# A mixture of experts: weights split in parts of 2048 columns instead of units of 1024, and in another order

## Chip, cores and metric

The kernel runs on one core of one Trainium2 chip. The metric is the time of one execution in microseconds of the device, as the median of several runs; less is better.

## What is computed

The reference is one inference step of a decoder layer for a prompt of 2048 tokens and 32 sample tokens: a mixer (attention and a state space part), and behind it a mixture of experts. Only the latter is touched by the change. Each token goes to two of 32 experts (one group of four, then two of its eight), and the tokens of an expert are worked in blocks of up to 128 rows:

```python
MOE_BLOCK = 128
...
    def expert_block(args):
        xb, e = args
        hid = jax.nn.silu(xb @ w_gate[e]) * (xb @ w_up[e])
        return hid @ w_down[e]
...
    contrib = ys[dest].astype(jnp.float32) * sg[:, None]
    return jax.ops.segment_sum(contrib, stok, num_segments=t)
```

Here `xb` is 128 x 1024, `w_gate` and `w_up` are 1024 x 512, and `w_down` is 512 x 1024, in float32, so an expert has 1.57 million weights, 6 MB.

## The kernel before

**Products out of high and low parts.** TensorE gets operands of the type float32r. Each float32 operand is split in two: `h` is its copy in that type (a cast on ScalarE, named ACT in the trace), and `l` the rest, `x - h` (a subtraction on VectorE, named DVE). A product is then three matmuls: h by h, h by l, l by h. `split` (L130) does this for tokens and hidden values: `xh, xl` of the block's tokens, `hh, hl` of the hidden values. The weights of an expert are split in the same way, by class `Experts` (L1888): loads of raw weights come in six tiles `raw0` to `raw5` of 128 x 2048 (0 to 3 hold gate and up, 4 and 5 hold down), each loaded by SyncE (SP) in `load_w` (L1874 for gate and up, L1877 for down). Each raw tile is split in two halves, so an expert has 12 units of 1024 columns: units 0 to 7 for the up products, 8 to 11 for the down products. `convert` (L1940 the cast, L1941 the subtraction) splits one unit into one of 16 places, and after the second half of a raw tile it issues the load of the next expert's weights into that tile. On SP this load waits for the subtraction to have read the tile.

**A block.** `block` (L2031) is one block of 128 tokens. TensorE first does the up products of both halves of the hidden columns for k = 0 to 3 (24 matmuls of 128 x 512, L2006), then the rest of half 0 (12). `act(0)` is Silu on ScalarE and the product on VectorE (hid, L2009 and L2010). `turned` transposes the next block's tokens (eight transposes, L1994). Then comes half 1 for k = 4 and 5, the two hid transposes of half 0 (`hidT`, L2014), which need the hid product, half 1 for k = 6 and 7, `act(1)`, the down products of c = 0 (six matmuls, L2023), the two hid transposes of half 1, and the down products of c = 1 to 3 (18). That is 72 matmuls. `store` (L2027) scales the result of the block before out of PSUM and sends it to memory. `prepare` splits the next block's tokens out of PSUM.

**What runs beside it.** An expert with up to 128 tokens has one block (`main`). One with more has up to three further blocks ahead of it (`further`), each under a branch (L2118, L2120, L2122). All of the splitting of the next expert's weights is written into the blocks of this expert as steps between the pieces of `block`: the last two units of this expert (`LATE`, down products c = 2 and 3) and the first four of the next (`EARLY`) go into the first further block, or, where there is none, into `main` under a branch of its own (`alone`, L2086, branch L2087). The other units go into `main` by the table `STEPS`. The order on every engine is the order in which the code is written (a manual schedule), so an instruction that waits holds up all that stands behind it on its engine. The first expert's weights are split ahead of this stage, in the tail of the router, by `late_split`.

Of the kernel before, what the change touches and what calls it, by code (L numbers as in the profile page):

```python
# [12 lines left out]
F32 = mybir.dt.float32  # L13
# [1867 lines left out]

STEPS = (), (0, 1, 2, 3, 4, 5), (6,), (7,), (), (), (8, 9)
EARLY = 0, 1, 2, 3
BOTH, AT0, AT1 = 4, 6, 1
LATE = 10, 11


class Experts:  # L1888
# [3 lines left out]
    UNITS, PLACES = 12, 16  # L1892
# [11 lines left out]
    def split(self, pool, *places):  # L1904

        for i in places:
            self.SP[i] = tuple(pool.tile([128, 1024], F32R, name=f"{nm}{i}") for nm in ("wh", "wl"))

    def load(self, p, i):
# [7 lines left out]
        if i in (0, 2, 5):  # L1917
            self.now = self.K.nc.sync.value_load(self.R.order[0:1, p:p + 1], min_val=0, max_val=31)
# [8 lines left out]
    def unit(self, p, u):  # L1927
        return self.SP[(self.UNITS * p + u) % self.PLACES]

    def convert(self, p, u, hi, lo):  # L1930

        h = u % 2
        raw = self.RAW[u // 2]
        wh, wl = self.unit(p, u)
        if u < 8:
            raw = raw.rearrange("p (j k f) -> p j k f", j=2, k=2)[:, :, h]
            wh, wl = (t.rearrange("p (j f) -> p j f", j=2) for t in (wh, wl))
        else:
            raw = raw[:, 1024 * h:1024 * h + 1024]
        hi(wh, raw)  # L1940
        lo.tensor_tensor(out=wl, in0=raw, in1=wh.bitcast(F32), op=ALU.subtract)  # L1941
        if h:
            self.load(p + 1, u // 2)


def moe(K, I, E, first, h2_d, Y_d, R, TK, last):
# [7 lines left out]
    with ExitStack() as st:  # L1954
        w = st.enter_context(tc.tile_pool(name="mw", bufs=1, reuse_waits="tile"))
        ps = st.enter_context(tc.tile_pool(name="mps", bufs=1, space=PSUM, reuse_waits="tile"))
        E.split(w, *range(8, E.PLACES))
        PT = [ps.tile([128, 4, 128], F32, name=f"pt{i}") for i in range(4)]
        PU = [ps.tile([128, 512], F32, name=f"pu{i}") for i in range(2)]
        PO = [ps.tile([128, 512], F32, name=f"po{i}") for i in range(2)]  # L1960
# [6 lines left out]
        for t in PO:  # L1967
            V.memset(t, 0.0)

        def convert(p, us):  # L1970
            for u in us:
                if p < NE:
                    E.convert(p, u, A.copy, V)
# [22 lines left out]
        def prepare():  # L1996

            for hf in range(2):
                ks = slice(4 * hf, 4 * hf + 4)
                split(K, XH[:, ks], XL[:, ks], PT[hf])  # L2000

        def up(p, hf, ks):
            for k in ks:
                wh, wl = (t.rearrange("p (j f) -> p j f", j=2)[:, :, 256 * hf:256 * hf + 256] for t in E.unit(p, k))
# [12 lines left out]
        def down(p, c):  # L2017
            wh, wl = E.unit(p, 8 + c)
# [6 lines left out]
        def store(col):  # L2025
            for i in range(2):
                A.activation(Y[:, 512 * i:512 * i + 512], PO[i], AF.Copy, scale=R.g[:, col:col + 1])  # L2027
# [3 lines left out]
        def block(p, before, x, steps, label, hint):  # L2031
# [28 lines left out]
            steps[6]()  # L2060
# [5 lines left out]

        def further(p, b):


            steps = [nothing] * 7  # L2070
            if b == 0:
                steps[0] = lambda: convert(p, LATE)
                steps[1] = lambda: convert(p + 1, EARLY)
# [10 lines left out]
        def main(p):  # L2084

            def alone():  # L2086
                with tc.If(blocks[p] <= 128):  # L2087
                    convert(p, LATE)
                    convert(p + 1, EARLY)

            def step(i):
                def run():
                    if i == 0:
                        alone()
                    elif i == 1:
                        gather_second(p + 1)
                    elif i == 2:
                        gather_first(p + 2)
                    convert(p + 1, [u for u in STEPS[i] if u not in EARLY])
                return run  # L2100

            block(p, 64 + p, X0 if p + 1 < NE else None, [step(i) for i in range(7)],
# [199 lines left out]
TK = 2176  # L2302
# [111 lines left out]
```

## Time and profile before

| | us |
|---|---|
| median of 3 runs | 2697.63 (2695.93 to 2702.63) |
| the profiled execution's own time | 2700.0 |
| its span | 2698.3 |
| expert stage, from 1627.3 to 2611.8 | 984.5 |
| TensorE busy in the span | 2441.5 (90%) |
| VectorE busy | 1435.3 (53%) |
| ScalarE busy | 1155.7 (43%) |

The mean granted clock of TensorE over the profiled execution is 0.951 of full speed. Times of the profile are counted from the start of the span. Matmuls overlap in the trace: a busy time of 0.4 us is that of one matmul from its start to its modelled end, while the next one starts 0.23 us later. A row of the timeline can stand for several instructions in a row (x6); what stands in brackets behind it is the time the engine stood idle ahead of it and what released it. `SPq` and `PEq` are the sequencers of SP and TensorE.

### The profile page before, as it was taken

The page shows a single profiled execution, that of the slowest core. Times are in us where ns is not written, and L with a number is a line of the kernel's source. Part 1 is how long each engine was busy: PE and PEld are TensorE (multiplying, and loading weights), DVE is VectorE, ACT ScalarE, POOL GpSimd, SP SyncE. Part 2 cuts the span into 40 slices and gives each one's busy share as a digit, 9 for nine tenths or more (in the row PEclk, how much of TensorE's full clock was granted, in tenths as well). Part 3 has the DMA queues.
Part 4 walks back from the last instruction along what each step waited for, and adds up shares of the span by engine and source line. Part 5 has one row for each costly group of instructions (what it writes and reads, how often), then busy time and mean ns, then how long its engine had stood idle before and what let it go on. Part 6 is the DMA issues. An engine that isn't in the chain of part 4 may idle for free. (4 is left out here: it accounts for less than half of the span.)

```text
span 2698.3 us, 36856 instructions
## 1 busy us (share of the span) xinstructions
PE 2441.5 (90%) x12135; PEld 1903.2 (71%) x12135; DVE 1435.3 (53%) x2977; ACT 1155.7 (43%) x1889; POOL 541.9 (20%) x712
## 2 busy tenths in 40 slices
PE   7999899897879999997999958999999999999987
PEld 3766677664457789996677736777777777777763
DVE  4444311256053566563677765537447566667528
ACT  3222211143143445645444435536446556666522
POOL 1022100001001334443344411111111111111103
PEclk9999999798889998998999968999999999999998
DMA  7322311466753632113433336547558577778657
GB/s 278 85 107 99 108 59 51 150 223 193 221 155 116 192 94 63 34 33 105 132 125 125 110 128 252 179 172 288 185 216 304 191 268 261 290 293 316 226 215 292
DMA packets 239281, 467.76 MB, mean 173 GB/s; under 512 B 87764, under 2 KB 117636, under 8 KB 236943
## 3 DMA queue, kind: packets, MB, share of 16 engines
q1 hardware_dynamic: 211496, 411.95, 44.2%
q0 software_dynamic: 16304, 38.50, 4.0%
q10 hardware_dynamic: 11200, 13.83, 1.5%
q8 instruction: 144, 2.36, 0.3%
q14 instruction: 137, 1.12, 0.1%
HBM read 395.60 MB, written 88.44 MB: 179 GB/s over the span
## 5 line engine op out<-in xcount | busy, mean ns | idle before, releaser
L1941 DVE TENSOR_TENSOR wl<-raw,wh 128x1024 fp32r<-128x1024 f32 x384 | 450.2, 1221 | 178.4 <-ACT wh L1940 177.8
L1940 ACT CAST wh<-raw 128x1024 fp32r<-128x1024 f32 x384 | 381.1, 1049 | 75.5 <-SPq L2118 58.8
L2006 PE MATMUL pu<-wh,xh 128*128 128x512 f32 x816 | 333.3, 408 | 20.8 <-PEq L2118 15.0
L2006 PE MATMUL pu<-wh,xl 128*128 128x512 f32 x816 | 323.1, 396 | 1.3 <-issue 1.3
L2006 PE MATMUL pu<-wl,xh 128*128 128x512 f32 x816 | 322.5, 395 | 0.0
L2028 POOL DMA_INDIRECT Y_d<-y,Rdst x52 | 66.8, 1285 | 764.9 <-ACT y L2027 731.6
L206 PE MATMUL po<-wh,hh 128*128 128x512 f32 x512 | 209.3, 409 | 12.1 <-ACT hh L133 12.1
L206 PE MATMUL po<-wl,hh 128*128 128x512 f32 x512 | 207.5, 405 | 0.0
L206 PE MATMUL po<-wh,hl 128*128 128x512 f32 x512 | 203.1, 402 | 0.0
L2006 PEld LDWEIGHTS pu<-wh,xh 128*128 128x128 f32 x816 | 154.5, 189 | 64.2 <-issue 34.3
L2006 PEld LDWEIGHTS pu<-wh,xl 128*128 128x128 f32 x816 | 154.3, 189 | 35.8
L873 DVE CUSTOM_DVE_ANT_0 jk<-pa,mask 128x256 bf16<-128x256 f32 (+1 forms) x384 | 118.0, 362 | 113.6 <-PE pa L870 112.7
L2006 PEld LDWEIGHTS pu<-wl,xh 128*128 128x128 f32 x816 | 154.6, 189 | 30.3
L2023 PE MATMUL po<-wh,hh 128*128 128x512 f32 x408 | 165.0, 404 | 0.0
L2023 PE MATMUL po<-wl,hh 128*128 128x512 f32 x408 | 160.5, 393 | 0.0
L2023 PE MATMUL po<-wh,hl 128*128 128x512 f32 x408 | 160.4, 393 | 0.0
L216 ACT COPY ob<-po 128x512 f32<-128x512 f32 x64 | 37.6, 587 | 266.2 <-PE po L206 264.3
L939 PE MATMUL pb<-QS,KH 128*128 128x256 f32 (+1 forms) x384 | 150.7, 399 | 0.0
L942 ACT ACTIVATE PT<-pb 128x512 f32<-128x512 f32 (+1 forms) x152 | 89.9, 591 | 122.2 <-PE pb L940 118.9
L940 PE MATMUL pb<-QM,KL 65*128 65x256 f32 (+1 forms) x384 | 139.6, 371 | 1.4 <-DMA QM<-MR 1.4
L2010 DVE TENSOR_TENSOR hid<-hid,pu 128x256 f32<-128x256 f32 x102 | 42.6, 417 | 184.1 <-ACT hid L2009 184.1
L988 PE MATMUL pw<-PT,vb 128*128 128x128 f32 (+1 forms) x752 | 132.1, 312 | 0.0
(588 smaller groups left out, 4973.4 us busy)
## 6 DMA issues: line engine op xcount, KB each, us to landing
raw<-w_expert_gate SPq DMA_DIRECT2D x128, 512.0 KB
raw<-w_expert_up SPq DMA_DIRECT2D x128, 512.0 KB
raw<-w_expert_down SPq DMA_DIRECT2D x64, 1024.0 KB
y<-Y_d SPq DMA_DIRECT2D x32, 512.0 KB
kr<-cache_k_win SPq DMA_DIRECT2D x56, 256.0 KB
kr<-cache_v_win SPq DMA_DIRECT2D x56, 256.0 KB
vb<-out_vp SPq DMA_DIRECT2D x96, 128.0 KB
wada<-w_ada_ffn SPq DMA_DIRECT2D x24, 512.0 KB
```

The costliest lines, as they stand in the source:

```text
L206: nc.tensor.matmul(out, a[:, kt, :], wt[c][:, kt], start=(kt == 0 and i == 0), stop=(kt == 7 and i == len(terms) - 1))
L873: V.tensor_tensor_reduce(out=jk[:, o:o + n], in0=pt[:, o:o + n], in1=mask[:, 256 - n:256], op0=ALU.add, op1=ALU.max, scale=1.0, scalar=-3e ...
L939: nc.tensor.matmul(po, cols(KH, c0, step, 128), cols(QS, c0, step, nq), start=True, stop=False)
L940: nc.tensor.matmul(po, cols(KL, c0, step, 128), cols(QM, c0, step, nq), start=False, stop=True)
L942: A.activation(PT[:, :o], ps[:, :o], AF.Exp)
L988: nc.tensor.matmul(out, vt[h, b, idx], PT[:, o + q0:o + q0 + n_], start=start, stop=(final and Wd == W), skip_group_check=True)
L1940: hi(wh, raw)
L1941: lo.tensor_tensor(out=wl, in0=raw, in1=wh.bitcast(F32), op=ALU.subtract)
L2006: nc.tensor.matmul(PU[hf], x[:, k, :], y, start=(k == 0 and j == 0), stop=(k == 7 and j == 2))
L2010: V.tensor_tensor(out=HID[hf], in0=HID[hf], in1=PU[hf][:, 256:512], op=ALU.mult)
L2023: nc.tensor.matmul(PO[i], x[:, c % 2, :], y[:, cs], start=(c == 0 and j == 0), stop=(c == 3 and j == 2))
L2028: nc.gpsimd.indirect_dma_start(out=Y_d, out_offset=bass.IndirectOffsetOnAxis(ap=R.dst[:, col:col + 1], axis=0), in_=Y, in_offset=None, bou ...
```

## The change

An expert's weights are split in six whole parts of 2048 columns, one per raw tile, into eight places, by one cast (`hi`) and one subtraction (`lo`) each. The tables of steps are replaced by four functions in `main`:

- `begin`: under the branch, parts 5 (of this expert), 0 and 1 (of the next). `further` does the same in its first block.
- `second`, ahead of the rest of half 0: the cast of part 2.
- `first`, behind the transposes of the next tokens: the subtraction of part 2, and the load into its tile.
- `end`, behind the second hid transposes: part 3 with its load, and part 4 without.

The load for part 4 is issued behind the next expert's branch L2118 and its further blocks, just ahead of its `main`. `AT0` goes from 6 to 7, so the first hid transposes stand behind three more up matmuls. `prepare` moves from ahead of the first down products to behind the second hid transposes, and splits all 1024 columns at once; `store` scales them at once. The loads for parts 4 and 5 each read the expert's number again. `late_split` does a whole part at every second call.

```diff
-STEPS = (), (0, 1, 2, 3, 4, 5), (6,), (7,), (), (), (8, 9)
-EARLY = 0, 1, 2, 3
-BOTH, AT0, AT1 = 4, 6, 1
-LATE = 10, 11
+LATE, EARLY = 5, (0, 1)
+BOTH, AT0, AT1 = 4, 7, 1
...
-    UNITS, PLACES = 12, 16
+    PARTS, PLACES = 6, 8
...
-        if i in (0, 2, 5):
+        if i in (0, 2, 4, 5):
             self.now = self.K.nc.sync.value_load(self.R.order[0:1, p:p + 1], min_val=0, max_val=31)
...
-        if h:
-            self.load(p + 1, u // 2)
...
+    def hi(self, p, i):
+        self.K.nc.scalar.copy(self.part(p, i)[0], self.RAW[i])
+
+    def lo(self, p, i):
+        wh, wl = self.part(p, i)
+        self.K.nc.vector.tensor_tensor(out=wl, in0=self.RAW[i], in1=wh.bitcast(F32), op=ALU.subtract)
...
+        def convert(p, *parts, hi=True, lo=True, load=True):
+
+            for i in parts:
                 if p < NE:
-                    E.convert(p, u, A.copy, V)
+                    if hi:
+                        E.hi(p, i)
+                    if lo:
+                        E.lo(p, i)
+                        if load:
+                            E.load(p + 1, i)
...
-            for hf in range(2):
-                ks = slice(4 * hf, 4 * hf + 4)
-                split(K, XH[:, ks], XL[:, ks], PT[hf])
+            split(K, XH, XL, PX)
...
-            for i in range(2):
-                A.activation(Y[:, 512 * i:512 * i + 512], PO[i], AF.Copy, scale=R.g[:, col:col + 1])
+            A.activation(Y, PY, AF.Copy, scale=R.g[:, col:col + 1])
...
             up(p, 1, range(AT0, 8))
-            steps[3]()
             act(1)
-            steps[4]()
-            if x is not None:
-                prepare()
-            steps[5]()
...
             hidT(1)
-            steps[6]()
+            if x is not None:
+                prepare()
+            steps[3]()
...
+        def early(p):
+            convert(p, LATE)
+            convert(p + 1, *EARLY)
...
-            def alone():
+            def begin():
                 with tc.If(blocks[p] <= 128):
-                    convert(p, LATE)
-                    convert(p + 1, EARLY)
...
+            def second():
+                gather_second(p + 1)
+                convert(p + 1, 2, lo=False)
+
+            def first():
+                gather_first(p + 2)
+                convert(p + 1, 2, hi=False)
+
+            def end():
+                convert(p + 1, 3)
+                convert(p + 1, 4, load=False)
...
+            if 0 < p:
+                E.load(p + 1, 4)
             main(p)
```

How this moves instructions shows at three places. The names: `wh`, `wl` with a number are the halves or parts of the split weights (`wh6` and `wh7` of before are the halves of part 3, `wh8` and `wh9` those of part 4, `wh10` is the first half of part 5), `hid` the hidden values, `pu` the PSUM of the up products, `px` (before `pt0` and `pt1`) that of the transposed tokens. The order lists don't tell when something runs.

The first place is VectorE in a last block, from the hid product of half 0 to the end. Before:

```order
L2010 TENSOR_TENSOR hid_13306<-hid_13306,pu0_13297 128x256
L1941 TENSOR_TENSOR wl6_12946<-raw3_12788,wh6_12945 128x1024
L134 TENSOR_TENSOR hl0_13308<-pt2_13295,hh0_13307 128x256
L1941 TENSOR_TENSOR wl7_12948<-raw3_12788,wh7_12947 128x1024
L2010 TENSOR_TENSOR hid_13306<-hid_13306,pu1_13298 128x256
L134 TENSOR_TENSOR xl_13302<-pt0_13293,xh_13301 128x512
L134 TENSOR_TENSOR xl_13302<-pt1_13294,xh_13301 128x512
L134 TENSOR_TENSOR hl1_13310<-pt3_13296,hh1_13309 128x256
L1941 TENSOR_TENSOR wl8_13278<-raw4_12791,wh8_13277 128x1024
L1941 TENSOR_TENSOR wl9_13280<-raw4_12791,wh9_13279 128x1024
```

And now:

```order
L2011 TENSOR_TENSOR hid_13280<-hid_13280,pu0_13272 128x256
L1939 TENSOR_TENSOR wl2_12942<-raw2_12785,wh2_12941 128x2048
L134 TENSOR_TENSOR hl0_13282<-pt2_13270,hh0_13281 128x256
L2011 TENSOR_TENSOR hid_13280<-hid_13280,pu1_13273 128x256
L134 TENSOR_TENSOR hl1_13284<-pt3_13271,hh1_13283 128x256
L134 TENSOR_TENSOR xl_13276<-px_13269,xh_13275 128x1024
L1939 TENSOR_TENSOR wl3_12944<-raw3_12788,wh3_12943 128x2048
L1939 TENSOR_TENSOR wl4_13262<-raw4_12791,wh4_13261 128x2048
```

The subtraction that stood in two halves of part 3 around `hl0` is now one of part 2 ahead of it; that of part 3 has gone behind `xl`, and `xl` behind `hl1`.

ScalarE in the same stretch, up to the branch L2118 of the next expert and the cast behind it, before:

```order
L1940 CAST wh6_12945<-raw3_12788 128x1024
L133 CAST hh0_13307<-pt2_13295 128x256
L1940 CAST wh7_12947<-raw3_12788 128x1024
L2009 ACTIVATE hid_13306<-pu1_13298 128x256
L133 CAST xh_13301<-pt0_13293 128x512
L133 CAST xh_13301<-pt1_13294 128x512
L133 CAST hh1_13309<-pt3_13296 128x256
L1940 CAST wh8_13277<-raw4_12791 128x1024
L1940 CAST wh9_13279<-raw4_12791 128x1024
L2082 TENSOR_LOAD Rcnt_79
L2118 COMPARE_AND_BRANCH
L1940 CAST wh10_13281<-raw5_12793 128x1024
```

And now:

```order
L2010 ACTIVATE hid_13280<-pu0_13272 128x256
L1990 UNCONDITIONAL_BRANCH
L133 CAST hh0_13281<-pt2_13270 128x256
L2010 ACTIVATE hid_13280<-pu1_13273 128x256
L133 CAST hh1_13283<-pt3_13271 128x256
L133 CAST xh_13275<-px_13269 128x1024
L1935 CAST wh3_12943<-raw3_12788 128x2048
L1935 CAST wh4_13261<-raw4_12791 128x2048
L2082 TENSOR_LOAD Rcnt_79
L2118 COMPARE_AND_BRANCH
L1935 CAST wh5_13263<-raw5_12793 128x2048
```

No cast of weights stands between the two Silu now; two casts of 2048 columns stand behind the cast of the tokens, which has moved behind `hh1`.

The third place is SP around that branch, and the casts behind it. SP before, with the semaphores on which an instruction waits:

```order
L1874 DMA raw3_12788<-w_expert_up 128x1024 [waits DMAHW7_49,DMAHW2_49]
L1877 ISA
L1877 DMA raw4_12791<-w_expert_down 128x2x1024 [waits DMAHW3_49,DMAHW0_49,DVE_49]
L2082 TENSOR_LOAD Rcnt_79
L2082 ISA x2
L2118 COMPARE_AND_BRANCH
```

SP now, ahead of the branch, and then behind it and the further blocks' code:

```order
L1874 ISA
L1874 DMA raw3_12788<-w_expert_up 128x1024 [waits DMAHW7_49,DMAHW2_49]
L2082 TENSOR_LOAD Rcnt_79
L2082 ISA x2
L2118 COMPARE_AND_BRANCH
```

```order
L1915 TENSOR_LOAD Rpre_93
L1915 ISA x2
L1877 ISA
L1877 DMA raw4_12791<-w_expert_down 128x2x1024 [waits DMAHW3_49,DMAHW0_49,DVE_49]
L2087 COMPARE_AND_BRANCH
```

The load into `raw4`, which waits for VectorE, has moved from ahead of the branch to behind it; the load of `raw3` stays ahead.

On ScalarE the casts of parts 5, 0 and 1 exist twice. Now, in the branch of an expert with more than one block (taken at L2118):

```order
L2118 COMPARE_AND_BRANCH
L1935 CAST wh5_13263<-raw5_12793 128x2048 [waits DMAHW4_49]
L1935 CAST wh6_13265<-raw0_12779 128x2048 [waits DMAHW6_49,DMAHW5_49,PE_49]
L1935 CAST wh7_13267<-raw1_12782 128x2048 [waits DMAHW0_49,DMAHW7_49,PE_49,Activation_49]
L2027 ACTIVATE y_13279<-po_13274,Rg_76 128x1024 [waits DMASW7_49,Activation_49]
```

And in that of an expert with one block, which comes by when the branch L2118 was skipped (taken at L2087):

```order
L2087 COMPARE_AND_BRANCH
L1935 CAST wh5_13263<-raw5_12793 128x2048 [waits DMAHW0_49,DVE_49,DMAHW4_49,PE_49,Activation_49]
L1935 CAST wh6_13265<-raw0_12779 128x2048 [waits DMAHW2_49,DMAHW5_49,DMAHW1_49,DMAHW6_49,DVE_49,Activation_49]
L1935 CAST wh7_13267<-raw1_12782 128x2048 [waits DMAHW4_49,DMAHW3_49,DMAHW7_49,DVE_49,Activation_49]
L2087 UNCONDITIONAL_BRANCH
```

The first copy of the cast of part 5 waits for a DMA queue alone; the second also waits for VectorE, TensorE and ScalarE itself.

## Rows read from the trace of the kernel before

**Rows 1.** Busy times by stretch: us, engines' busy us (instructions), PEclk, DMA share, GB/s.

```profile
1627.30:2611.80 984.50, 938.83 (x4276) 749.20 (x4276) 574.48 (x681) 549.61 (x785) 132.56 (x100) 0.99 0.66 241
...
2014.90:2033.70 18.80, 18.30 (x84) 14.52 (x84) 9.96 (x12) 9.08 (x14) 2.02 (x2) 1.00 0.45 155
2033.70:2053.70 20.00, 18.64 (x85) 14.56 (x85) 16.44 (x18) 14.99 (x20) 2.65 (x2) 1.00 0.86 316
2053.70:2073.40 19.70, 18.52 (x84) 14.68 (x85) 16.57 (x19) 16.57 (x22) 4.80 (x3) 1.00 0.95 355
2073.40:2091.40 18.00, 18.00 (x85) 14.77 (x84) 9.66 (x12) 8.20 (x14) 1.25 (x1) 1.00 0.80 314
```

**Rows 2.** Waits from 1650 to 2600 us: total us, times, longest us.

```profile
ACT wh L1940 <- SPq L2118: 58.8, 18, 4.1
...
PE pt L2014 <- DVE hid L2010: 24.4, 47, 1.9
...
PE pu L2006 <- PEq L2118: 9.0, 19, 2.9
```

**Rows 3.** Groups by form, whole span: busy us, mean ns | idle us before.

```profile
L1941 DVE TENSOR_TENSOR wl<-raw,wh 128x1024 fp32r<-128x1024 f32 x384 | 450.2, 1221 | 178.4 <-ACT wh L1940 177.8
...
L1940 ACT CAST wh<-raw 128x1024 fp32r<-128x1024 f32 x384 | 381.1, 1049 | 75.5 <-SPq L2118 58.8 <-PE pu L2006 12.2 <-PEq L2118 4.5
...
L2006 PE MATMUL pu<-wh,xh 128*128 128x512 f32 x816 | 333.3, 408 | 20.8 <-PEq L2118 15.0 <-PEq L2120 3.9 <-PEq L2122 1.9
...
L134 DVE TENSOR_TENSOR xl<-pt,xh 128x512 fp32r<-128x512 f32 x102 | 65.4, 683 | 1.1
...
L134 DVE TENSOR_TENSOR wl<-wraw,wh 128x512 fp32r<-128x512 f32 x32 | 20.1, 682 | 0.6 <-ACT wh L133 0.5
...
L133 ACT CAST wh<-wraw 128x512 fp32r<-128x512 f32 x32 | 17.5, 621 | 4.3 <-DMA wraw<-w_in 4.3
```

**Rows 4.** Timeline of PE in a block of an expert with one block.

```profile
2033.74 0.47 PE L2006 MATMUL pu<-wh,xh 128*128 128x512 f32 x1 [0.30 <-PEq L2118]
...
2045.34 0.44 PE L2014 MATMUL pt<-ident,hid 128*128 128x128 f32 x2 [0.71 <-DVE hid L2010]
...
2048.83 0.44 PE L2014 MATMUL pt<-ident,hid 128*128 128x128 f32 x2 [0.31 <-DVE hid L2010]
```

**Rows 5.** Timeline of DVE around that block.

```profile
2030.69 2.36 DVE L1941 TENSOR_TENSOR wl<-raw,wh 128x1024 fp32r<-128x1024 f32 x2 [0.41 <-ACT wh L1940]
...
2035.75 9.20 DVE L1941 TENSOR_TENSOR wl<-raw,wh 128x1024 fp32r<-128x1024 f32 x8 [2.69 <-ACT wh L1940]
2044.87 0.41 DVE L2010 TENSOR_TENSOR hid<-hid,pu 128x256 f32<-128x256 f32 x1
```

**Rows 6.** Timeline of ACT around that block.

```profile
2034.66 5.79 ACT L1940 CAST wh<-raw 128x1024 fp32r<-128x1024 f32 x6 [3.05 <-SPq L2118]
...
2054.86 5.79 ACT L1940 CAST wh<-raw 128x1024 fp32r<-128x1024 f32 x6 [3.23 <-SPq L2118]
```

**Rows 7.** Timeline of PE in a block that waits for nothing.

```profile
2073.42 0.39 PE L2006 MATMUL pu<-wh,xh 128*128 128x512 f32 x1
...
2083.97 0.38 PE L2014 MATMUL pt<-ident,hid 128*128 128x128 f32 x2
...
2085.59 0.39 PE L2023 MATMUL po<-wh,hh 128*128 128x512 f32 x1
...
2086.99 0.38 PE L2014 MATMUL pt<-ident,hid 128*128 128x128 f32 x2
```

**Rows 8.** Timelines of ACT, then DVE, in that block.

```profile
2084.44 0.37 ACT L133 CAST hh<-pt 128x256 fp32r<-128x256 f32 x1 [2.19 <-PE pt L2014]
...
2084.85 0.42 DVE L134 TENSOR_TENSOR hl<-pt,hh 128x256 fp32r<-128x256 f32 x1 [2.14 <-ACT hh L133]
```

**Rows 9.** Busy times by stretch: a long wait of PE, and what follows.

```profile
1954.90:1958.30 3.40, 0.54 (x4) 0.30 (x2) 0.00 (x0) 0.43 (x1) 0.00 (x0) 1.00 1.01 392
1958.40:1961.70 3.30, 3.30 (x10) 2.52 (x9) 2.76 (x3) 3.30 (x5) 0.00 (x0) 0.50 0.70 274
```

**Rows 10.** Timeline of PE behind that wait.

```profile
1958.30 0.57 PE L2006 MATMUL pu<-wl,xh 128*128 128x512 f32 x1
...
1961.65 0.45 PE L2006 MATMUL pu<-wh,xh 128*128 128x512 f32 x1
```

More of the change, by code (lines that the diff above doesn't have):

```diff
@@ L1906, in split @@
         for i in places:
-            self.SP[i] = tuple(pool.tile([128, 1024], F32R, name=f"{nm}{i}") for nm in ("wh", "wl"))
+            self.SP[i] = tuple(pool.tile([128, 2048], F32R, name=f"{nm}{i}") for nm in ("wh", "wl"))
     def load(self, p, i):
@@ L1925, in begin, with part, up, down @@
             self.load(p, i)
[L1927 to L1941, printed above, removed]
-        if h:
-            self.load(p + 1, u // 2)
+    def part(self, p, i):
+        return self.SP[(self.PARTS * p + i) % self.PLACES]
+    def up(self, p, k, hf):
+        return [t.rearrange("p (j k f) -> p j k f", j=2, k=2)[:, :, k % 2, 256 * hf:256 * hf + 256] for t in self.part(p, k // 2)]
+    def down(self, p, c):
+        return [t[:, 1024 * (c % 2):1024 * (c % 2) + 1024] for t in self.part(p, 4 + c // 2)]
+    def hi(self, p, i):
[3 more added lines that the diff above has]
+        self.K.nc.vector.tensor_tensor(out=wl, in0=self.RAW[i], in1=wh.bitcast(F32), op=ALU.subtract)
 def moe(K, I, E, first, h2_d, Y_d, R, TK, last):
@@ L1956, in moe @@
         ps = st.enter_context(tc.tile_pool(name="mps", bufs=1, space=PSUM, reuse_waits="tile"))
-        E.split(w, *range(8, E.PLACES))
-        PT = [ps.tile([128, 4, 128], F32, name=f"pt{i}") for i in range(4)]
+        E.split(w, *range(4, E.PLACES))
+        PX = ps.tile([128, 8, 128], F32, name="px")
+        PT = [PX[:, 0:4], PX[:, 4:8]] + [ps.tile([128, 4, 128], F32, name=f"pt{i}") for i in range(2, 4)]
         PU = [ps.tile([128, 512], F32, name=f"pu{i}") for i in range(2)]
-        PO = [ps.tile([128, 512], F32, name=f"po{i}") for i in range(2)]
+        PY = ps.tile([128, 1024], F32, name="po")
+        PO = [PY[:, 0:512], PY[:, 512:1024]]
         XH, XL = (w.tile([128, 8, 128], F32R, name=f"x{nm}") for nm in "hl")
@@ L2017, in down @@
         def down(p, c):
-            wh, wl = E.unit(p, 8 + c)
+            wh, wl = E.down(p, c)
             hh, hl = HT[c // 2]
@@ L2065, in nothing @@
             pass
+        def early(p):
+            convert(p, LATE)
+            convert(p + 1, *EARLY)
         def further(p, b):
-            steps = [nothing] * 7
+            steps = [nothing] * 4
             if b == 0:
-                steps[0] = lambda: convert(p, LATE)
-                steps[1] = lambda: convert(p + 1, EARLY)
+                steps[0] = lambda: early(p)
             else:
@@ L2084, in main @@
         def main(p):
-            def alone():
+            def begin():
                 with tc.If(blocks[p] <= 128):
-                    convert(p, LATE)
-                    convert(p + 1, EARLY)
[L2091 to L2102, printed above, removed]
+                    early(p)
+            def second():
[7 more added lines that the diff above has]
+                convert(p + 1, 4, load=False)
+            block(p, 64 + p, X0 if p + 1 < NE else None, (begin, second, first, end),
                   f"at128_{p + 1}" if p + 1 < NE else None, blocks[p + 1] > 128 if p + 1 < NE else None)
@@ L2106, in moe @@
         E.begin()
-        convert(0, range(first, min(LATE)))
+        convert(0, *range(first, LATE))
         gather_second(0)
@@ L2376, in late_split @@
                 for u in range(done[0], min(done[0] + n, 8)):
-                    E.convert(0, u, nc.scalar.copy, nc.vector)
+                    if u % 2:
+                        E.hi(0, u // 2)
+                        E.lo(0, u // 2)
+                        E.load(1, u // 2)
                     done[0] = u + 1
@@ L2383, in program @@
             with tc.manual_schedule():
-                moe(K, I, E, done[0], h2_d, Y_d, R, TK, last)
+                moe(K, I, E, done[0] // 2, h2_d, Y_d, R, TK, last)
             with tc.manual_schedule():
```

11 lines of the change are left out of this document (4 added, 7 removed).

## The prediction

> **What bounds the kernel now.** I read the busy table by stretch first. In the expert stage TensorE is busy 938.8 of 984.5 us, VectorE 574.5, ScalarE 549.6, the DMA engines 0.66 of the time [rows 1]. So TensorE sets the time of this stage, and only its 46 idle us can be won or added to. The other stages hardly change. The 816 first up products of a kind [rows 3] are 816/16 = 51 blocks for 32 experts: 19 are further blocks, 32 are last ("main") blocks. The 19 waits of TensorE behind the branch of L2118 [rows 2] are one for each skipped branch, so 20 experts (with the first, which shows no such wait) have one block, and 12 have more. I call the former singles.
>
> Four blocks in a row show what each kind costs [rows 1]: the last block of an expert with several 18.8 us, two singles 20.0 and 19.7, an undisturbed block 18.0. A single is long because all the splitting of the next expert falls on one block: VectorE is busy 16.4 of 20.0 us there. The timelines say where it hurts. ScalarE stands idle 3.05 us before the cast of the part 5 halves, put down to SP's branch [rows 6], and 18 such waits sum to 58.8 us [rows 2]. VectorE, which waits for these casts, idles 2.69 us, then does eight subtractions in 9.20 us, and only then the hid product at 2044.87 [rows 5]. TensorE waits 0.71 us for it at the first hid transpose and 0.31 at the second [rows 4]. The sum of such waits is 24.4 us in 47 [rows 2]; it is this that the change can move.
>
> **Sizes.** A cast of 512 columns takes 621 ns, of 1024 columns 1049; a subtraction 682 and 1221 [rows 3]. Going on in a straight line, 2048 columns cost 1049 + 2 x 428 = 1.9 us and 1221 + 2 x 539 = 2.3 us. In a row they cost less: six casts take 5.79 us [rows 6], eight subtractions 9.20 [rows 5], so about 1.8 and 2.2 us for 2048. A pair of halves thus saves about 0.1 us on ScalarE and 0.06 on VectorE: work for the engines hardly falls, and what counts is the order.
>
> **Where the splitting goes.** Before, VectorE had one half of part 3 (1.2 us) between the hid product of half 0 and hl0, and the other ahead of the product of half 1. Now three things are different. The whole subtraction of part 2 (2.3 us) stands between the hid product of half 0 and hl0; parts 3 and 4 come at the end of the block, behind hl1 and xl; and the split of x has moved behind the second hid transpose.
>
> I walk the last block of an expert with several, times from its first matmul. An undisturbed block has hid transposes at 10.55 and 13.57 and the first down product at 12.17 [rows 7]. The second hid transposes come 0.17 later (below), at 13.74; hh1 ends at 14.6, the x cast (1.05) at 15.65, the x subtraction (1.22) at 16.95, the cast of part 3 at 17.45, its subtraction at 19.8, that of part 4 at 22.0. The block is 18.2 us plus 0.4 for a branch, 18.6. So VectorE ends **3.3 us into the next block**; before, the last two subtractions began at 2030.69 and ended 0.7 us ahead of it [rows 5].
>
> **A single after that.** The cast of part 5 stands in a branch of its own. On the path where it is skipped, VectorE makes up its counts when it passes; the cast on the path taken for the next block waits for VectorE's earlier count. In the program, the copy of this cast behind a skipped first branch waits for VectorE; the copy in the branch of an expert with several blocks waits for its load alone. So in a single the cast starts at 3.5, not when SP is through: 3.5 to 5.4, part 0 to 7.2, part 1 to 9.0, the store (one of 1024) to 10.1, part 2 to 11.9, Silu to 12.25, product to 12.65. The first hid transposes stand at 12.7, where the block of before has 2045.34 - 2033.74 = 11.6 [rows 4]; the new order alone would put them at 11.25. Then the subtraction of part 2 holds VectorE till 14.95 and hl0 till 15.35, so the third down product starts at 15.6; the first two, on hh, end their turn at 14.25. This wait of 1.35 us is **new**. The second hid transposes follow four matmuls later, at 16.5, against 2048.83 - 2033.74 = 15.1 [rows 4]: 1.4 us later. A second walk, calibrated on both blocks of before (it puts that transpose at 15.2), gives 1.1. I take 1.25, so 20.0 becomes 21.3 and 19.7 becomes 20.9, and the delay into the next block (3.3 us) repeats itself. Times 19: **+23.8 us**, bounds 20.9 and 26.6.
>
> **The other terms.** AT0 = 7 moves the first hid transposes behind three more matmuls of 0.233 us (six from 2085.59 to 2086.99 [rows 7]), from 10.55 to 11.25, while hh is cast 0.47 us after them (2084.44 - 2083.97 [rows 7, 8]) in 0.37 us, and hl takes 0.42 more [rows 8]; 0.06 us lie between the end of a hid product (2044.87 + 0.41 [rows 5]) and the transposes that wait for it [rows 4]; since hh has to be loaded as weights first I take 0.25, and the first down product starts at 11.25 + 0.47 + 0.37 + 0.25 = 12.34 instead of 12.17. That is 0.17 us in a block without other waits; bounds 0 (with 0.06 us) and 0.25. For the 19 further blocks +3.2 us; in the 12 last blocks it is in the 18.6 above, which makes them 0.2 shorter than 18.8: -2 us. The tail of the router (eight subtractions of 1.22 become four of 2.3, -0.6) and the last store in one (+0.4) give -0.2. The first block has no predecessor: 0, give or take 1. The load of part 4 goes out behind the next branch instead of ahead of it, with one value load more on SP: part 4 is wanted first at the end of the block, some 15 us on, and loads move in 0.86 to 0.95 of the DMA time of a single [rows 1], so I put it at nothing; if that cover is gone, the cast of part 4 waits, which is behind everything that TensorE waits for in that block.
>
> Sum: 23.8 + 3.2 - 2 - 0.2 = +24.8 us on the profiled run's 2700.0, so 2724.8; that run is 2.4 above the median of the three shown, so **2722 us**.
>
> The Trainium skill ("Perfetto Trace Analysis", section Optimizing Scalar/DVE Operations) says that grouping into larger operations helps throughput where the engine is saturated, and that where Scalar or Vector are not saturated but cause bubbles on other engines, "breaking up instructions may allow work to be completed sooner". Its first half is the fourth rival; its second half goes with the forecast.
>
> **Rivals.** (1) *The clock falls too.* After TensorE stood still for 2.9 us at 1954.9 to 1958.3 the granted clock fell to 0.50 for 3.3 us [rows 9], the lower of the two levels. Nine matmuls took 1961.65 - 1958.30 = 3.35 us [rows 10] where 9 x 0.233 = 2.1 would do: 1.25 us lost. Should two waits of 1.3 us close together do as one of 2.9, singles lose that too: all 19 make +24, half of them +12: 2734 to 2746. Against it: the waits of 0.7 and 0.3 in a single leave the clock at 1.00 [rows 1].
> (2) *The delay is smaller.* If the split of x or part 3 ends 1.2 us sooner than walked, the carry is 2 us, half of the waits goes, and 19 x 0.5 + 1 = +10 at most, 0 at least: 2692 to 2706. For it: each step of the walk is a mean of rows from elsewhere.
> (3) *Faster: the cast of part 5 is not held.* Today it is SP that comes late, since it waits for VectorE before it issues the load of part 4; the change takes that load from ahead of the branch. If the cast starts as soon as SP is through, at about the block's start, casts run 3 us earlier, VectorE idles nowhere, the hid product is on time and a single costs 18.9 or 18.45: -1.15 x 19 = -22, 2676 by that, 2685 if the loads set the pace (at 392 GB/s they fill the engines to 1.01 [rows 9], and a single already moves 355 [rows 1]). It decides from the point where this cast starts before the subtraction of part 4 ends. Against it stands the wait in the program.
> (4) *Grouping is all that happens.* Saving 0.06 to 0.1 us on each of six pairs, 0.45 us per single, and no new wait: -9, 2689. Mechanism: the 9.20 us ahead of the hid product shrink by that much. The rule is in the sentence above on the Trainium skill.
>
> **Chances.** Forecast (2711 to 2733, which takes in the bounds above) 0.62; clock 0.07; smaller delay 0.15; faster 0.12; grouping 0.04. The range leaves out the faster case, the grouping case, and the upper half of the clock case, 0.2 in all: 2692 to 2740. About 0.3% (8 us) is what a measurement of this kernel can tell from no change: faster by more 0.14 (with half of the grouping case), within it 0.17, slower 0.69.
>
> **What would show it.** In the profile after: singles of 21.3 and 20.9 us and last blocks of 18.6; VectorE's subtraction of part 4 ending some 3 us into a single, with the cast of part 5 released by VectorE and not by SP; a new wait of TensorE for hl of 1.35 us at the third down product, about 19 times, and 1.0 us more at the first hid transposes; casts of 1.9 and subtractions of 2.3 us; further blocks of 18.2. The prediction is wrong if the cast of part 5 starts within a microsecond of the block's start (rival 3), if the wait for hl is under 0.5 us (rival 2), or if the granted clock of the singles is below 1.00 (rival 1).

## The result, and the profile after

The changed kernel takes 2758.86 us (median of 4 runs, 2755.53 to 2763.48) against 2696.82 (4 runs, 2695.93 to 2702.63): a ratio of 1.0227, with a 95% interval of 1.0206 to 1.0247. It is 2.3% slower, 62 us; forecast were 25 us, and a range up to 2740. The profiled execution has a span of 2761.8 us and a mean granted clock of 0.935 (before 0.951).

First the busy times by stretch, in the columns of [rows 1]: the expert stage, then the last block of an expert with several, two singles, and a block that waits for nothing.

```profile
1625.70:2674.30 1048.60, 964.92 (x4276) 768.52 (x4276) 563.52 (x445) 521.65 (x496) 189.91 (x100) 0.96 0.63 227
2030.00:2051.90 21.90, 18.21 (x84) 14.50 (x85) 9.61 (x8) 8.54 (x9) 3.80 (x2) 1.00 0.29 101
2051.90:2075.60 23.70, 19.86 (x85) 15.72 (x85) 16.32 (x11) 14.38 (x13) 5.52 (x2) 0.93 0.85 307
2075.60:2095.30 19.70, 19.70 (x84) 15.81 (x85) 12.53 (x10) 13.29 (x12) 6.55 (x3) 0.91 0.93 339
2095.30:2113.40 18.10, 18.10 (x85) 14.62 (x84) 13.22 (x10) 9.92 (x10) 1.30 (x1) 1.00 0.79 287
```

The stage grew by 64 us, from 984.5 to 1048.6; all of the loss lies here. The block that waits for nothing is 18.1 us instead of 18.0. From its start to that of the next block, the last block of an expert with several now takes 21.9 us and a single 23.7 where the next expert is a single too; the wait ahead of that next block is counted in. The single behind which no single comes takes 19.7. The granted clock inside singles is 0.91 to 0.93 where it was 1.00. The waits at the branch are these (list of waits, 1650 to 2670 us: total, times, longest):

```profile
PE pu L2007 <- DVEq L2118: 71.3, 19, 3.8
...
ACT wh L1935 <- DVEq L2118: 38.3, 13, 2.9
...
ACT wh L1935 <- SPq L2118: 20.0, 6, 4.0
```

TensorE's first up product waits 3.75 us for VectorE's sequencer at the branch L2118, in each of the 19 singles behind the first. In [rows 2] this place had 9.0 us in 19. ScalarE's wait for SP has shrunk from 58.8 us in 18 places [rows 2] to 20.0 in 6, and VectorE has taken SP's place in the other 13 (38.3 us). The waits of the hid transposes for VectorE, 24.4 us in [rows 2], are gone.

One of these places in the timeline, all engines:

```profile
2047.22 4.50 DVE L1939 TENSOR_TENSOR wl<-raw,wh 128x2048 fp32r<-128x2048 f32 x2 [0.58 <-ACT wh L1935]
...
2047.81 0.40 PE L2024 MATMUL po<-wh,hl 128*128 128x512 f32 x1
...
2051.92 0.47 PE L2007 MATMUL pu<-wh,xh 128*128 128x512 f32 x1 [3.71 <-DVEq L2118]
2051.93 5.51 ACT L1935 CAST wh<-raw 128x2048 fp32r<-128x2048 f32 x3 [2.94 <-DVEq L2118]
...
2053.54 0.63 PE L2007 MATMUL pu<-wh,xl 128*128 128x512 f32 x1
...
2053.97 0.63 PE L2007 MATMUL pu<-wh,xh 128*128 128x512 f32 x1
```

The subtractions of parts 3 and 4 end at 2051.72; TensorE's last down product began at 2047.81, and 0.2 us after VectorE is through, TensorE and ScalarE start together. Then the up products stand 0.43 us apart instead of 0.233. The busy times show the clock there:

```profile
2052.60:2056.00 3.40, 3.40 (x10) 2.69 (x9) 2.13 (x1) 3.40 (x3) 0.00 (x0) 0.51 0.98 330
```

Why TensorE waits stands in the program. An engine that skips a branch adds to its semaphore what the skipped code would have added, and only when its own earlier work is through. What stands behind the branch waits for the sum. For the second expert (W is the value of a semaphore that an instruction waits for, U what it adds):

```
DVE EventSemaphore  W[DVE>=1862] U[DVE+=18]
PE EventSemaphore  W[DVE>=1876] U[]
PE Matmult pu0_13272 W[Activation>=1057] U[]
PE Matmult pu0_13272 W[DVE>=1880] U[]
```

1862 is reached when the subtraction of part 4 has ended, and 1862 + 18 = 1880. Of VectorE's results the first up products need only what was long done (the split tokens `xl` above all); but the count by which they wait for it comes behind the branch. The first product waits for ScalarE's made-up count as well (1057); VectorE's comes last.

Where the stage's 64 us come from, worked out from the starts of all its matmuls (time from one start to the next, less 0.2325 us after a matmul of 512 columns and 0.13 after a transpose), in us. The medians are of the runs, the other columns of one profiled execution each; the kernels below "changed" are those of the next section:

| kernel | median us | before a block's first matmul | its first 16 up products | ahead of hid transposes | among down products |
|---|---|---|---|---|---|
| before | 2697 | 19.4 | 4.2 | 32.6 | -2.3 |
| changed | 2759 | 83.2 | 34.5 | -2.2 | 2.4 |
| lo4_behind | 2716 | 42.6 | 1.6 | 6.0 | 22.0 |
| filled | 2735 | (16.2) | 15.5 | -2.2 | 2.1 |
| load4_ahead | 2761 | 83.1 | 33.4 | -2.2 | 2.4 |
| at0_6 | 2762 | 82.9 | 36.2 | -0.2 | -2.5 |
| order_alone | 2746 | 70.4 | 22.9 | 8.3 | -2.4 |
| size_alone | 2737 | 24.7 | 4.0 | 61.0 | -0.9 |
| size_load4 | 2708 | 25.8 | 2.0 | 36.9 | -2.4 |
| load4_only | 2679 | 20.1 | 4.9 | 13.0 | -2.4 |
| load4_lo7 | 2673 | 18.8 | 2.6 | -1.9 | 10.0 |
| balanced | 2768 | 19.7 | 2.5 | 74.9 | 24.1 |
| balanced2 | 2713 | 20.7 | 3.2 | 22.4 | 18.8 |

From before to changed: +63.8 of waits ahead of blocks, +30.3 of slow first products, -34.8 of waits at the hid transposes, +4.7 among the down products, together +64.0.

### The profile page after: what moved, and what is told of

Same layout as the page of the kernel before. It is cut to its first block, busy times and chain, and to the rows that moved or that the text cites. A ratio compares the mean times of both kernels' runs of the same rounds, so it can differ in the third digit from the quotient of the medians.

```text
span 2761.8 us, 36165 instructions
## 1 busy us (share of the span) xinstructions
PE 2468.3 (89%) x12135; PEld 1923.5 (70%) x12135; DVE 1424.3 (52%) x2733; ACT 1127.6 (41%) x1594; POOL 599.0 (22%) x712
## 5 line engine op out<-in xcount | busy, mean ns | idle before, releaser
L1939 DVE TENSOR_TENSOR wl<-raw,wh 128x2048 fp32r<-128x2048 f32 x192 | 430.4, 2287 | 74.1 <-ACT wh L1935 74.1
L2007 PE MATMUL pu<-wh,xh 128*128 128x512 f32 x816 | 346.5, 425 | 85.1 <-DVEq L2118 71.3
L1935 ACT CAST wh<-raw 128x2048 fp32r<-128x2048 f32 x192 | 355.1, 1909 | 82.6 <-DVEq L2118 38.3
L2007 PE MATMUL pu<-wl,xh 128*128 128x512 f32 x816 | 335.5, 411 | 0.0
L2007 PE MATMUL pu<-wh,xl 128*128 128x512 f32 x816 | 335.3, 411 | 0.0
L2028 POOL DMA_INDIRECT Y_d<-y,Rdst x52 | 89.6, 1723 | 758.3 <-ACT y L2027 729.9
L2007 PEld LDWEIGHTS pu<-wh,xh 128*128 128x128 f32 x816 | 162.4, 199 | 130.2 <-issue 97.0
L2007 PEld LDWEIGHTS pu<-wh,xl 128*128 128x128 f32 x816 | 161.9, 198 | 38.5
L2007 PEld LDWEIGHTS pu<-wl,xh 128*128 128x128 f32 x816 | 162.8, 200 | 33.0
```

Of the source, the lines that this page charges most:

```text
L1935: self.K.nc.scalar.copy(self.part(p, i)[0], self.RAW[i])
L1939: self.K.nc.vector.tensor_tensor(out=wl, in0=self.RAW[i], in1=wh.bitcast(F32), op=ALU.subtract)
L2007: nc.tensor.matmul(PU[hf], x[:, k, :], y, start=(k == 0 and j == 0), stop=(k == 7 and j == 2))
L2028: nc.gpsimd.indirect_dma_start(out=Y_d, out_offset=bass.IndirectOffsetOnAxis(ap=R.dst[:, col:col + 1], axis=0), in_=Y, in_offset=None, bou ...
```

## The experiments

The diffs are cut (...), and the comments in them are added here.

### Is it VectorE's last subtraction that holds TensorE? (lo4_behind)

```diff
         def early(p):
+            if p:
+                convert(p, 4, hi=False)
             convert(p, LATE)
...
             def end():
                 convert(p + 1, 3)
-                convert(p + 1, 4, load=False)
+                convert(p + 1, 4, lo=False)
...
-            if 0 < p:
-                E.load(p + 1, 4)
```

> Only the subtraction of part 4 (and the load behind it) moves, from the end of the block to behind the next branch, ahead of that of part 5. Theory A (TensorE itself waits, behind a skipped branch, for VectorE's count, which VectorE makes up only when its last subtraction of the block before is through; the clock falls after this wait): VectorE now passes the branch when part 3 is through, some 1.4 us behind the block's end instead of 3.7, so the 19 waits shrink to about 1.5 us and the clock stays up: 2759 - 19 x (2.2 + 1.7) = 2685, plus up to 1.3 us in each single for the late hid product or hl0: 2685 to 2710. Theory B (what costs is the subtraction of part 2 ahead of hl0, or SP's load behind the branch): nothing moves, 2750 to 2765.

Measured: 2715.98 us (ratio to the kernel before 1.0076, 1.0059 to 1.0093), 43 us less than the changed kernel. From its list of waits:

```profile
ACT wh L1935 <- SPq L2120: 53.0, 16, 4.6
DVE wl L1939 <- SPq L2120: 48.5, 18, 4.0
...
PE pu L2007 <- DVEq L2120: 26.5, 17, 1.6
...
PE po L2024 <- DVE hl L134: 14.9, 18, 0.9
```

The wait at the branch (here L2120) goes from 71.3 to 26.5 us and the slow products go (1.6 us left of 34.5). So VectorE's work left over at the branch is the cause, and the clock follows the wait (the load that moves along makes no difference, see load4_ahead). It came out 6 us above the expected range. With TensorE early again, waits come back that the changed kernel doesn't have: 8.2 us at the hid transposes and 19.6 among the down products. Most of the latter is a wait that the prediction had put into the changed kernel, 0.8 us at the third down product, 18 times, for `hl`, behind the subtraction of part 2. ScalarE and VectorE also wait for SP behind the branch here (the first two lines), which the expectation left out; how much of the 6 us comes from that was not tested.

### What does the clock cost? (filled)

```diff
+            if p + 1 < NE:
+                with tc.If(blocks[p + 1] <= 128):
+                    fill(p)     # 14 x nc.tensor.matmul(PU[0], ...)
```

> The changed kernel, with 14 more matmuls of 128x512 (3.3 us, into a PSUM tile that nobody reads) behind the last down product of a block, where the next expert has one block. They lie in the wait of 3.9 us for VectorE. Theory F (about 1.4 to 1.9 us of each of the 19 singles are lost to the clock, which falls after that wait): the granted clock of the singles goes up to 1.00 and 19 x 1.5 = 29 us come back, less up to 0.4 us for the extra branch in 31 blocks: 2730 to 2745. Theory F' (the clock costs nothing): 2757 to 2772.

Measured: 2734.7 us (1.0155, 1.0135 to 1.0176), inside the range of theory F. Two singles by busy times:

```profile
2059.20:2082.20 23.00, 21.66 (x99) 16.96 (x97) 17.14 (x12) 15.09 (x13) 6.08 (x3) 1.00 0.90 317
2037.20:2059.20 22.00, 21.55 (x100) 17.14 (x99) 16.20 (x12) 14.26 (x13) 5.27 (x2) 1.00 0.85 301
```

The granted clock is back at 1.00 with TensorE busy through the wait, and 24 us come back although VectorE is through no sooner (the table counts the 14 products as the singles' own, hence the bracket, and what is left of the wait behind them stands in the next column; counted from the first up product itself the two columns are 29.8 and 2.3, so the slow products are gone in all 19 singles). So 24 us of the loss, at least, are the clock's, and at most 38 the wait's, net of what the late start saves.

### Is it the load behind the branch, or AT0? (load4_ahead, at0_6)

```diff
-                convert(p + 1, 4, load=False)
+                convert(p + 1, 4)
...
-            if 0 < p:
-                E.load(p + 1, 4)
```

> The changed kernel, with the load of part 4 issued ahead of the branch again, as before. If VectorE's passing is the gate in the changed kernel (theory A), TensorE waits as long as now, and only the first cast of a single comes some 1.5 us later, which a single that starts late and slow hides in part: 2757 to 2775. If the load behind the branch were what costs (theory B), the time would fall below 2745.

Measured: 2761.29 us (1.0245, 1.0228 to 1.0263), no different from the changed kernel's 2758.86. ScalarE's wait for SP at the branch is 84.9 us there, and TensorE's for VectorE 71.4, as in the changed kernel: where VectorE is the gate, it doesn't matter when SP comes.

The other edit is `AT0` from 7 to 6.

> The changed kernel with AT0 back at 6. By the prediction's term a block without other waits gets 0.17 us shorter (18.02 instead of 18.13 to 18.2), 51 x 0.1 to 0.17 = 5 to 9 us, unless the singles, which begin late and slow, wait elsewhere for it: 2750 to 2757. If the three matmuls ahead of the transposes hide VectorE's late hid product in the changed kernel, 2760 or more.

Measured: 2762.05 us (1.0234, 1.0214 to 1.0253), no different either. The table shows 4.9 us less among the down products and 1.7 and 2.0 more elsewhere. The time lies in the expectation's second range, but the waits at the hid transposes are only 2.0 us longer, so a late hid product explains little of it. So the prediction's term of 3.2 us for the further blocks is not seen in the time.

### Size or order? (order_alone, size_alone)

The kernel before, with its units of 1024 and the new order at the end of a block:

```diff
-STEPS = (), (0, 1, 2, 3, 4, 5), (6,), (7,), (), (), (8, 9)
+STEPS = (), (0, 1, 2, 3, 4, 5), (), (), (), (), (6, 7, 8, 9)
...
             hidT(1)
+            if x is not None:
+                prepare()
             steps[6]()
```

> The kernel before with its units of 1024 columns, with the new order at the end of the block alone: units 6 to 9 (parts 3 and 4) behind the second hid transposes and behind the split of the tokens. Theory A: order is what costs; VectorE ends some 4 us into a single, TensorE waits for it 19 times and the clock falls: 2755 to 2770. Theory C (whole parts are to blame, since a cast of 1.9 us lets the subtraction start later): under 2725.

Measured: 2745.89 us (1.0191, 1.0174 to 1.0208), five runs between 2724.48 and 2750.22 whose mean granted clock is 0.954 in the shortest and 0.936 to 0.947 in the others. In the profiled one, the shortest:

```profile
PE pu L2006 <- DVEq L2118: 58.8, 19, 3.2
```

The same wait, 3.1 us each. In this execution the clock fell behind 13 of the 19 waits and not behind the other 6, where it fell behind all 19 in the changed kernel. That the number of falls differs from run to run fits the spread of times and mean clocks, but only this run was profiled. The median lies 9 us below the expected range; the shortest run comes down to the 2725 of the other theory, but with this wait in it. So the order alone makes the wait, with small units too.

Whole parts, in about the order of before (part 3 cast behind the first Silu, subtracted ahead of the product of half 1; the rest as it was):

```diff
+                convert(p + 1, 3, lo=False)   # first
...
+            steps[4]()                        # subtraction of part 3
             act(1)
+            if x is not None:
+                prepare()
...
-                convert(p + 1, 3)
-                convert(p + 1, 4, load=False)
+                convert(p + 1, 4)
```

> Whole parts of 2048 columns in about the order of before: part 2 ahead of the first Silu, part 3 around the first hid transposes and ahead of the product of half 1, the tokens' split ahead of the down products, part 4 at the end with its load, six k ahead of the first hid transposes. Theory A: VectorE ends about at the block's end, no long wait at the branch, and the product of half 1 is up to 1 us late in 31 blocks: 2695 to 2725. Theory C (whole parts are to blame): 2740 or more.

Measured: 2737.06 us (1.0147, 1.013 to 1.0164), between the two ranges. Its list of waits:

```profile
PE pt L2015 <- DVE hid L2011: 53.0, 46, 2.2
...
PE pu L2007 <- DVEq L2118: 10.9, 17, 0.7
```

No long wait for VectorE at the branch, but the hid product is late: 53.0 us where [rows 2] has 24.4, in the same places. The order and the durations say why: a subtraction starts only when the whole cast of 1.9 us ahead of it has ended, and the product of half 1 stands behind one of 2.3 us instead of 1.2; ScalarE's wait for SP also grows, from 58.8 us [rows 2] to 73.0. This kernel has the store and the tokens' split in one piece too, and what they do alone was not tested. So each half of the change costs on its own, 49 us for the order and 40 for the size, and together 62. They don't add up: in the changed kernel, where TensorE starts late, the waits for the hid product are gone (-2.2 in the table).

### What is the load behind the branch worth by itself? (load4_only, size_load4)

The kernel before with this edit alone (and with the expert's number read again ahead of the load):

```diff
-        if h:
+        if h and (p == 0 or u // 2 != 4):
             self.load(p + 1, u // 2)
...
+            if 0 < p:
+                E.load(p + 1, 4)
             main(p)
```

> The kernel before with one edit: the load of part 4 is issued behind the next branch, just ahead of main, as the change does. Theory D: before, ScalarE's first cast of a single waits for SP, which can pass the skipped branch only after it has issued this load, and that waits for VectorE's last subtraction of the block (SP issues at 2033.08, the cast starts at 2034.66). With the load behind the branch the cast waits for VectorE's own passing alone, some 1.3 us sooner; the first hid product is on time, the 0.9 to 1.3 us ahead of the first hid transposes go in the singles: 2697 - 19 x 1 = 2678, up to 2688 if loads set the pace. Theory D': SP is not what the cast waits for; 2690 to 2703.

Measured: 2678.84 us (0.9936, 0.9919 to 0.9953), 18 us faster than before. Timeline of one single, which begins at 2028.9:

```profile
2028.21 4.39 SPq L1877 DMA_DIRECT2D raw<-w_expert_down  x2
...
2028.75 5.80 ACT L1940 CAST wh<-raw 128x1024 fp32r<-128x1024 f32 x6 [2.01 <-PEq L2118]
...
2029.83 9.21 DVE L1941 TENSOR_TENSOR wl<-raw,wh 128x1024 fp32r<-128x1024 f32 x8 [1.64 <-ACT wh L1940]
```

Busy times of this single and the one behind it:

```profile
2028.90:2047.90 19.00, 18.38 (x85) 14.60 (x85) 16.52 (x18) 15.01 (x21) 2.65 (x2) 1.00 0.89 333
2047.90:2066.50 18.60, 18.34 (x84) 14.75 (x85) 16.70 (x19) 16.54 (x22) 4.81 (x3) 1.00 0.98 366
```

ScalarE's first cast starts some 0.13 us ahead of the block's start, where it stood 0.9 us behind it [rows 4, 6]; VectorE idles 1.64 us instead of 2.69 [rows 5]; the two singles take 19.0 and 18.6 us instead of 20.0 and 19.7 [rows 1]. The DMA engines are busy 0.98 of the second, so loads could soon set the pace; no run here tests it.

The same edit on size_alone (`load=False` for part 4, and the load ahead of `main`):

> The kernel 'size_alone' (whole parts in about the order of before) with the load of part 4 behind the next branch as well. If the load's gain (some 18 us with units of 1024) is one of the first cast of a single only, it comes back here too, since the singles of 'size_alone' wait about 2 us at the first hid transposes: 2737 - 19 x 1.3 = 2712, down to 2705. If whole parts cost for another reason than a late chain of cast, subtraction and hid product, the time stays over 2725.

Measured: 2707.51 us (1.0045, 1.0024 to 1.0066), 30 us below size_alone, more than the 25 expected. The waits ahead of the hid transposes fall from 61.0 to 36.9 us. The load's place is worth it with either size, as long as VectorE is not late.

### A kernel that beats both, and one that doesn't (load4_lo7, balanced, balanced2)

load4_only with the subtraction of unit 7 behind the product of half 1:

```diff
+                    if i in (3, 4) and p + 1 < NE:
+                        E.convert(p + 1, 7, A.copy, V, "hi" if i == 3 else "lo")
```

> The kernel 'load4_only', with the subtraction of unit 7 moved from ahead of the product of half 1 to behind it (its cast stays). In 31 blocks the second hid transposes wait 0.4 us for that product, since VectorE does the 1.2 us of unit 7 first. If nothing takes the place of this wait: 2679 - 31 x 0.4 = 2667. If the tokens' split and unit 9, which follow on VectorE, end that much later and TensorE waits for them at the branch instead: 2675 to 2682.

Measured: 2672.57 us (0.9912, 0.9895 to 0.9929), the fastest here. This lies between the two forecasts. The waits ahead of the hid transposes go (from 13.0 to -1.9), and 12.4 us among the down products come, most of them waits of some 0.3 us for the second `hl` in 30 blocks (VectorE then does unit 7 and the tokens' split ahead of it), with 3.6 us less in the table's other two columns; the median falls by 6 us, half of what was hoped.

Before that I had tried to keep whole parts and even out VectorE: parts 3 and 4 subtracted behind the branch, part 2 behind the product of half 1, part 3 cast behind the first Silu.

```diff
         def early(p):
+            if p:
+                convert(p, 3, 4, hi=False)
...
             act(1)
+            steps[4]()      # convert(p + 1, 2, hi=False)
```

> The subtractions of parts 3 and 4 stand behind the branch, that of part 2 behind the product of half 1, and the cast of part 3 behind the first Silu, so that neither VectorE nor ScalarE has work left at the block's end. Theory A: VectorE and ScalarE pass the branch ahead of TensorE; the 19 waits at the branch go back to 0.3 to 0.5 us, VectorE does five subtractions from the block's start (11.2 us), and the first hid product is late by about half a us: singles of 18.6 to 19.2 us, 2670 to 2690, if loads don't set the pace; 2690 to 2700 if they do. Theory B': the gain of the grouping is nothing and the order can't beat the one before: 2697 or more.

Measured: 2768.16 us (1.0269, 1.0252 to 1.0286), slower than all others and some 70 us over the range expected. Its waits at the branch are short, but VectorE stands idle behind it:

```profile
DVE wl L1939 <- SPq L2120: 102.6, 18, 7.1
```

and in one single, from the load of part 2 (on SP) on:

```profile
2066.60 1.34 SPq L1874 DMA_DIRECT2D raw<-w_expert_up  x1
...
2075.23 8.90 DVE L1939 TENSOR_TENSOR wl<-raw,wh 128x2048 fp32r<-128x2048 f32 x4 [6.97 <-SPq L2120]
```

In the program SP, too, makes up the counts of the skipped loads, and for each count it waits until the transfer that runs under it has landed. The landings in this trace show it: from 2069.85 to 2074.94 SP makes up five counts, each within 0.03 us of the landing of a load. The last of these loads is that of part 2, issued at 2066.60 and landed at 2074.91; VectorE starts at 2075.23. In the next experiment the load of part 2 was put behind the branch as well:

```diff
+            if 0 < p:
+                E.load(p + 1, 2)
             main(p)
```

> As the kernel 'balanced', but the load of part 2 too is issued behind the next branch. In 'balanced' VectorE stood idle for up to 7 us behind the branch until SP had passed it. Theory E: SP passes a skipped branch only after the loads on the queues that it makes up have landed, and the load of part 2 had been issued at the block's end; with it behind the branch VectorE starts at once, and singles are 18.6 to 19.4 us: 2675 to 2700. Theory E': it waits for something else, and the time stays at 2750 to 2775.

Measured: 2713.01 us (1.0066, 1.005 to 1.0083), 55 us less than balanced, but 13 us over the expected range. VectorE's wait for SP (the second line) fell to 37.7 us:

```profile
ACT wh L1935 <- DMA raw<-w_expert_up: 39.1, 28, 4.0
DVE wl L1939 <- SPq L2120: 37.7, 8, 5.6
```

Of the 9 first singles behind an expert with several blocks, 7 take 18.8 to 18.9 us now, as expected, and two 20.1 and 21.1. Second ones take 20.4 to 24.4: SP still waits there for the landings of earlier loads (at 2050.44, 2052.01 and 2053.40 in one single), and casts also wait for loads that are issued late (the first line). So it is landings that hold SP, and in balanced that of part 2's load came last in the single shown.

## Why the prediction was wrong

**The direction and the cause's first half were right.** VectorE does end late: 3.3 us into a single were forecast (22.0 less 18.6 in its own walk is 3.4), 3.7 are measured (2051.72 against 2048.04, the last down product's start plus 0.23). Casts take 1.91 us and subtractions 2.29, as extrapolated (groups by form, after):

```profile
L1939 DVE TENSOR_TENSOR wl<-raw,wh 128x2048 fp32r<-128x2048 f32 x192 | 430.4, 2287 | 74.1 <-ACT wh L1935 74.1
L1935 ACT CAST wh<-raw 128x2048 fp32r<-128x2048 f32 x192 | 355.1, 1909 | 82.6 <-DVEq L2118 38.3 <-PE pu L2007 24.3 <-SPq L2118 20.0
```

ScalarE's cast of part 5 is held by VectorE in 13 singles, as said; in the other 6 the list still names SP. The load's new place costs nothing in the changed kernel (load4_ahead).

**The step that failed is the first line of the walk through a single.** It lets TensorE begin its up products at the block's start and holds only the cast of part 5 until 3.5 us. I had found the wait for VectorE's count in the program for the cast, and did not ask for whom else that count stands. The first up product waits for it just so, 3.75 us on average in 19 singles. That is +63.8 us ahead of blocks that the sum did not have. The trace of before doesn't have this wait: VectorE's last subtraction ends ahead of the block's end there [rows 5], and all 19 waits at this branch are put down to TensorE's own sequencer [rows 2]. The long one among them, ahead of the slow products of [rows 9], is no exception:

```profile
1952.45 2.36 DVE L1941 TENSOR_TENSOR wl<-raw,wh 128x1024 fp32r<-128x1024 f32 x2 [0.41 <-ACT wh L1940]
...
1957.99 0.47 PE L2006 MATMUL pu<-wh,xh 128*128 128x512 f32 x1 [2.86 <-PEq L2118]
```

VectorE is through at 1954.81, 3.2 us ahead of TensorE's start. So the wait for VectorE had to be found in the changed program, by asking of TensorE's first instruction behind the branch what had been asked of ScalarE's.

**The term of +23.8 us did not come.** The 1.05 us at the first hid transposes and the 1.35 us at the third down product come from VectorE's delay against a TensorE that is on time; with TensorE held as long as VectorE they vanish, and with them the 32.6 us of waits of before. The second is real where TensorE is early: lo4_behind has it, at 0.8 us, 18 times. The direction came out right, but by waits other than those that were added up.

**The clock was a rival with the right mechanism and the wrong trigger.** I gave it 0.07, for two waits of 1.3 us. What came was one wait of 3.7 us in each of 19 singles, longer than that of [rows 9], and 30.3 us of slow products, 1.6 for each single where 1.25 was the estimate; filled gives 24 of them back. Once a wait of over 3 us was foreseen, the clock would have belonged in the sum, since the trace of before had one case, behind a wait of 2.86 us.

**"Work for the engines hardly falls, and what counts is the order" was half right.** The size alone costs 40 us (size_alone), which the sum put at nothing: larger pieces are done later, though they take no longer in sum. Work did fall as little as was said, by 11 us on VectorE and 28 on ScalarE in the stage. The Trainium skill ("Perfetto Trace Analysis", section Optimizing Scalar/DVE Operations) says that breaking up instructions may complete work sooner where the engine isn't saturated but causes bubbles on others; size_alone agrees, with 53.0 us of waits for the hid product against 24.4 and VectorE busy about half of the time. The grouping rival (2689) did not happen.

**Small terms.** AT0: 0.1 us in a further block (18.1 against 18.0) for the 0.17 forecast, and nothing in the time of at0_6. The last blocks of experts with several were to be 18.6; they are 18.0 and a wait of 3.9.

**The rival "faster" was a good account of another kernel.** Its price, 2676 to 2685, is what load4_only gives (2679) with that part of the change alone. Its condition, the cast not held behind VectorE's leftover work, is what the rest of the change breaks.

## What to carry to other kernels

In a program that makes up counts in this way, work that an engine has not finished when it comes to a skipped branch holds every engine that waits for a later count of it behind that branch, even for data that was ready long before: find the last work of each engine ahead of a branch, and ask of all engines, TensorE first, who waits for its count behind it. When a change has parts, price each alone: here, of the three that were priced, one gained 18 us, and the other two lost 49 and 40. Larger pieces saved little here, where they cost nearly in proportion (a subtraction of 2048 columns 2287 ns, two of 1024 columns 2 x 1221), and delayed what waited for a piece.

## What was not expected of the hardware

A wait of TensorE of 3.7 us was followed by the lower clock in all 19 singles of the changed kernel behind it (0.51 over 3.4 us in the one shown), 7 to 13 products some 0.43 us apart. In lo4_behind no such run of slow products follows the 18 waits of some 1.7 us, and in order_alone waits of 3.2 us had either outcome, 13 times and 6; its runs spread over 26 us. Fourteen products that nobody needs, put into the wait, made the kernel 24 us faster.
